# The order and the width of the twelve matmuls of a weight slot

## The chip, the cores and the metric

The kernel runs on one core of a Trainium2 chip. The metric is the device time of one execution in microseconds (us). Several executions are made, and the median is taken. One further execution is profiled; all rows below are from that one.

## What is computed

The reference is the trunk of an encoder: four layers over 256 tokens of width 2048, with a cross-attention to 256 memory rows. Cut to what matters here:

```python
for i in range(DEPTH):                      # 4 layers
    h = rms_norm(x, norm_g[i])              # 256 x 2048
    z = h @ w_in                            # 2048 x (5632 or about 7168)
    mix_out = (gmlp, forgetting attention, differential attention)[i % 3](z)
    kv = mem_n @ w_mem_kv[i]                # 256 x 2048 @ 2048 x 1024
    mem_out = memory_attention(...)
    branch = concatenate([mix_out, mem_out]) * silu(gate)
    x = x + branch @ w_out[i]               # 2048 x 2048
```

All inputs are float32. Nearly all of the arithmetic lies in the three kinds of product with a weight matrix: `w_mem_kv`, `w_in` and `w_out`.

## The kernel before

**Chunks and slots.** Each weight matrix is cut into blocks of 512 output columns, the chunks. There are 74 of them in the program, numbered here from 0 in the order in which they run: 0 to 7 are the memory keys and values, 8 to 18 the input projection of layer 0, 19 to 22 its output projection, 23 to 36 and 37 to 40 those of layer 1, 41 to 54 and 55 to 58 those of layer 2, 59 to 69 and 70 to 73 those of layer 3. `chunk_product` (L148) runs one chunk. A chunk has eight slots; a slot is a weight tile of 128 partitions by 1024 elements, which holds two blocks of 128 rows of the matrix (`kk` is 0 or 1), each 512 columns wide.

**The split in three products.** Every float32 operand is split in two parts of the type float32r, a high one and a low one. ScalarE makes the high part of the weights (`whi`, L117), VectorE the low part (`wlo`, L118), for the slot that is four ahead. The activations lie transposed as `xh` and `xl` (for the input projections) or `bh` and `bl` (for the memory rows and the output projections). One product is then three matmuls, one per term: `xh` with `whi` (L173), `xh` with `wlo` (L174) and `xl` with `whi` (L175). The activations are the stationary operand, 128 by 128, and the weights are the moving operand, 512 columns. The 256 tokens make two token tiles (`t` is 0 or 1), each with its own accumulator `acc[t]`, one bank of PSUM. So a slot has 2 (`kk`) x 2 (`t`) x 3 (terms) = 12 matmuls, and the program has 74 x 8 x 12 = 7104 of them. Before each one the chip loads its stationary operand: the trace has one weight load (the row PEld) for each matmul (the row PE).

**What sets the order.** The order on each engine is the order in which the program issues (a manual schedule). Within a slot it is `for kk, t in order`, with the three terms innermost; in the last slot of a chunk (`n == 7`) `order` is sorted by `t`, so that `acc[0]` is complete six matmuls ahead of `acc[1]`. Between slots `between_slots` (L142) issues whatever else is due: transposes, small matmuls of the attention, the next weight load on SyncE's queue (`load_until`), the next split (`split_until`). Four raw tiles, four `whi` and four `wlo` are the buffers; a `whi` buffer comes free when the last matmul that reads it is done, and the ScalarE instruction that refills it waits for that.

**Other matmuls.** Transposes (L344, L551, L560, L611, L799), scores (L459, L476, L501) and the gating product (L677) are float32 matmuls that stand between slots. A float32 matmul is run by the chip in two passes, each with a record of its own. The forget gate (L714 to L716) is the one other place with float32r: its stationary operand has 12 columns and its moving operand 256.

Of the kernel before, what the change touches and what calls it, by code (L numbers as in the profile page):

```python
# [24 lines left out]
CW = 512  # L25
# [7 lines left out]
RAW_BUFS = 4  # L33
PART_BUFS = 4
WARM = 10
LAM_LAYER = 2
LAM_INIT = 0.8 - 0.6 * math.exp(-0.3 * LAM_LAYER)

# [4 lines left out]
def trunk_kernel(  # L43
# [23 lines left out]
    nc = tc.nc  # L67
# [26 lines left out]

    pieces = piece_sequence()
    raws, parts, first_raw = {}, {}, []
    state = {"slot": 0, "raw": 0, "part": 0}

    def load_until(n):
        while state["raw"] < min(n, len(pieces)):  # L100
# [28 lines left out]
    def tick():  # L129
        for gen in list(tasks):  # L130
            if next(gen, tasks) is tasks:
                tasks.remove(gen)
        tasks.extend(fresh)
        fresh.clear()

    def run_late():
        todo = list(late)
        late.clear()
        for fn in todo:
            fn()  # L140

    def between_slots():  # L142
        tick()
        split_until(state["slot"] + PART_BUFS)
        load_until(state["slot"] + PART_BUFS + RAW_BUFS)
        run_late()

    def chunk_product(parts_of):  # L148
        acc = [
            ps_acc.tile([P, CW], F32, tag="acc", name=f"acc{t}") for t in range(2)  # L150
        ]
        for n in range(8):
            between_slots()
            slot = state["slot"]
            kp = pieces[slot][1]
            guard = 0
            while parts_of(kp) is None:
                assert (tasks or fresh) and guard < 100
                tick()
                run_late()  # L160
                guard += 1
            xh, xl = parts_of(kp)
            hi, lo = parts.pop(slot)
            order = [(kk, t) for kk in range(2) for t in range(2)]
            if n == 7:
                order.sort(key=lambda o: o[1])
            for kk, t in order:
                first = n == 0 and kk == 0
                last = n == 7 and kk == 1
                wh = hi[:, kk * CW : (kk + 1) * CW]  # L170
                wl = lo[:, kk * CW : (kk + 1) * CW]
                c = slice(kk * S + t * P, kk * S + (t + 1) * P)
                nc.tensor.matmul(acc[t], xh[:, c], wh, start=first, stop=False)  # L173
                nc.tensor.matmul(acc[t], xh[:, c], wl, start=False, stop=False)  # L174
                nc.tensor.matmul(acc[t], xl[:, c], wh, start=False, stop=last)  # L175
            state["slot"] += 1
        return acc


# [7 lines left out]
    warm_ps = ps_t.tile([P, CW], F32, tag="t", name="warm_ps")  # L187
    for _ in range(WARM):
        nc.tensor.matmul(warm_ps, warm[:, :P], warm, start=True, stop=True)
# [18 lines left out]
    def transposed_load(src, kp):  # L208
        raw = tmp.tile([P, 2 * S], F32, tag="xo", name="xraw", bufs=4)
        nc.sync.dma_start(raw, src[kp])  # L210
        return raw
# [21 lines left out]
    raw = tmp.tile([P, 2 * S], F32, tag="xo", name="xraw", bufs=4)  # L233
    m_hi, m_lo = new_parts("b", 0)
    bparts[0] = (m_hi, m_lo)
    for k in range(2):
        nc.sync.dma_start(raw[:, k * S : (k + 1) * S], mem_t[0, :, k * S : (k + 1) * S])
        w = slice(k * CW, (k + 1) * CW)
        nc.sync.dma_start(w_raw[:, w], pieces[0][0][0, :, w])
    for k in range(2):  # L240
        c, w = slice(k * S, (k + 1) * S), slice(k * CW, (k + 1) * CW)
# [3 lines left out]
    for kp in range(1, early):  # L245
        raw = transposed_load(mem_t, kp)
# [115 lines left out]
    for i in range(DEPTH):  # L362
        acc = chunk_product(lambda kp: bparts[kp])
        vv = heads.tile([P, 2, CW], F32, tag="vv", name="mvv")

        def store_values(i=i, acc=acc, vv=vv):
            scaled_rows(acc, r_mem, vv)
            nc.gpsimd.dma_start(mv_d[i], vv.rearrange("p a b -> p (a b)"))

        if i == 0:  # L370

            def first_values():
                yield from token_rms(mem, r_mem)
                yield
                store_values()

            spawn(first_values())
        else:
            store_values()
        if i == 2:  # L380
            spawn(load_transposed(x_t, "x", 0, xparts))
        if i == 3:
            spawn(token_rms(x, r_x))
        acc = chunk_product(lambda kp: bparts[kp])
        kt = heads.tile([P, 4, S], F32, tag="kT", name="mkt")

        def store_keys(i=i, kt=kt):
            nc.gpsimd.dma_start(mk_d[i], kt.rearrange("p a b -> p (a b)"))

        spawn(norm_task(acc, r_mem, gains[:, G_MK + i : G_MK + i + 1], HD, kt, store_keys))  # L390
# [415 lines left out]
    for i in range(DEPTH):  # L806
# [9 lines left out]
        def product():  # L816
            return chunk_product(lambda kp: xparts[kp])
# [26 lines left out]
        if kind == 0:  # L844
# [3 lines left out]
            for c in range(3):  # L848
                acc = product()
# [9 lines left out]
            for c in range(3):  # L859
                acc = product()  # L860
# [6 lines left out]
        else:  # L867
# [10 lines left out]
            for c in range(3):  # L878
                ready = []
                acc = product()  # L880
                qt = heads.tile([P, 4, S], F32, tag="qT", name="qt")
                spawn(norm_task(acc, r_x, qgains[:, gq : gq + 1], width, qt))
                acc = product()
# [11 lines left out]
                acc = product()  # L895
# [27 lines left out]
        for n in range(4):  # L923
            xo = old_rows(i, n)
            acc = chunk_product(lambda kp: bnext[kp])
# [90 lines left out]
```

## Time and profile before

| what | value |
|---|---|
| median of 3 runs | 1813.2 us (1813.01 to 1814.32) |
| the profiled execution: its time | 1813.01 us |
| its span (first to last instruction) | 1810.9 us |
| what lies around the span | 2.1 us |
| PE busy | 1791.0 us, 99% of the span |
| DVE busy / ACT busy | 1020.9 us / 905.4 us |
| mean granted TensorE clock | 0.994 |

PE is TensorE's matmul row, PEld its weight loads, which overlap it; DVE is VectorE, ACT ScalarE, POOL GpSimd, SP SyncE. A matmul's recorded duration reaches beyond the start of the next one, since matmuls are pipelined: the pace at which they run is read from start to start, not from the duration.

### The profile page before, as it was taken

The page shows a single profiled execution, that of the slowest core. Times are in us where ns is not written, and L with a number is a line of the kernel's source. Part 1 is how long each engine was busy: PE and PEld are TensorE (multiplying, and loading weights), DVE is VectorE, ACT ScalarE, POOL GpSimd, SP SyncE. Part 2 cuts the span into 40 slices and gives each one's busy share as a digit, 9 for nine tenths or more (in the row PEclk, how much of TensorE's full clock was granted, in tenths as well). Part 3 has the DMA queues.
Part 4 walks back from the last instruction along what each step waited for, and adds up shares of the span by engine and source line. Part 5 has one row for each costly group of instructions (what it writes and reads, how often), then busy time and mean ns, then how long its engine had stood idle before and what let it go on. Part 6 is the DMA issues. An engine that isn't in the chain of part 4 may idle for free.

```text
span 1810.9 us, 22215 instructions
## 1 busy us (share of the span) xinstructions
PE 1791.0 (99%) x8290; PEld 1465.7 (81%) x8290; DVE 1020.9 (56%) x1431; ACT 905.4 (50%) x1273; POOL 113.4 (6%) x131
## 2 busy tenths in 40 slices
PE   8999999999899999999999999999999999999999
PEld 6888888887688888888888887878888888888887
DVE  5456557554455555555555555766565555755454
ACT  5546545543455545455544454555464444554432
POOL 0110100000000110000000100101000000100000
PEclk9999999999899999999999999999999999999999
DMA  8767765556776455555566645454546766545564
GB/s 273 269 224 264 248 218 178 185 177 158 201 232 218 163 178 183 165 173 175 197 218 229 204 161 188 153 172 161 177 151 216 230 222 222 166 163 182 185 221 164
DMA packets 103932, 355.97 MB, mean 197 GB/s; under 512 B 12064, under 2 KB 12364, under 8 KB 103696
## 3 DMA queue, kind: packets, MB, share of 16 engines
q1 hardware_dynamic: 97344, 332.97, 55.3%
q0 software_dynamic: 5760, 20.50, 4.0%
q8 instruction: 65, 1.06, 0.3%
q10 hardware_dynamic: 720, 1.09, 0.2%
q14 instruction: 43, 0.35, 0.1%
HBM read 339.55 MB, written 14.95 MB: 196 GB/s over the span
## 4 chain that ended last, share of the span: by engine, by line
PE 96%; DMA 3%; ACT 0%; DVE 0%; issue 0%; SPq 0%; ACTq 0%; DVEq 0%
PE acc L173 30%; PE acc L175 29%; PE acc L174 29%; PE tb L551 2%; DMA raw<-in_w_o_dram 2%; PE tb L344 1%; PE tb L560 1%; PE tb L611 1%; PE s L459 1%; PE s L501 1%; PE tb L799 1%; PE sv L677 1%; DMA xraw<-in_mem_t_dram 1%; DMA raw<-in_w_kv_dram 1%; PE s L476 0%; ACT whi L117 0%
## 5 line engine op out<-in xcount | busy, mean ns | idle before, releaser
L118 DVE TENSOR_TENSOR wlo<-raw,whi 128x1024 fp32r<-128x1024 f32 x591 | 722.8, 1224 | 629.8 <-ACT whi L117 623.5
L117 ACT CAST whi<-raw 128x1024 fp32r<-128x1024 f32 x591 | 619.3, 1048 | 544.0 <-PE acc L175 472.8
L173 PE MATMUL acc<-whi,xh 128*128 128x512 f32 x1600 | 647.1, 404 | 2.6 <-ACT whi L117 2.6
L175 PE MATMUL acc<-whi,xl 128*128 128x512 f32 x1600 | 629.1, 393 | 0.0
L174 PE MATMUL acc<-wlo,xh 128*128 128x512 f32 x1600 | 625.0, 391 | 0.8 <-DVE wlo L118 0.8
L175 PEld LDWEIGHTS acc<-whi,xl 128*128 128x128 f32 x1600 | 300.9, 188 | 68.9
L173 PEld LDWEIGHTS acc<-whi,xh 128*128 128x128 f32 x1600 | 301.4, 188 | 67.3 <-issue 3.2
L174 PEld LDWEIGHTS acc<-wlo,xh 128*128 128x128 f32 x1600 | 301.5, 188 | 62.4 <-DVE wlo L118 1.1
L173 PE MATMUL acc<-whi,bh 128*128 128x512 f32 x768 | 306.2, 399 | 6.3 <-ACT whi L117 3.5
L174 PE MATMUL acc<-wlo,bh 128*128 128x512 f32 x768 | 303.5, 395 | 2.8 <-DVE wlo L118 1.8
L175 PE MATMUL acc<-whi,bl 128*128 128x512 f32 x768 | 301.5, 393 | 0.4 <-DVE bl L199 0.4
L173 PEld LDWEIGHTS acc<-whi,bh 128*128 128x128 f32 x768 | 145.4, 189 | 39.8 <-ACT whi L117 5.3
L174 PEld LDWEIGHTS acc<-wlo,bh 128*128 128x128 f32 x768 | 145.6, 190 | 34.0 <-DVE wlo L118 3.1
L175 PEld LDWEIGHTS acc<-whi,bl 128*128 128x128 f32 x768 | 145.4, 189 | 33.1 <-DVE bl L199 1.1
L307 POOL TENSOR_TENSOR sc<-sc,expo 128x8 f32<-128x8 f32 (+1 forms) x23 | 56.8, 2469 | 543.7 <-DVE sc L306 477.4
L564 ACT COPY pt<-tb 128x256 f32<-128x256 f32 (+1 forms) x80 | 27.2, 340 | 125.5 <-PE tb L560 125.3
L199 DVE SCALAR_TENSOR_TENSOR xl<-tb,gk,xh 128x256 fp32r<-128x256 f32 x48 | 23.2, 484 | 29.5 <-ACT xh L198 29.4
L198 ACT ACTIVATE xh<-tb,gk 128x256 fp32r<-128x256 f32 x48 | 22.8, 475 | 32.6 <-PE tb L799 19.4
L615 ACT CAST bh<-tb 128x512 fp32r<-128x512 f32 x26 | 15.3, 588 | 47.5 <-PE tb L611 47.5
L781 POOL DMA_DIRECT2D x_d<-xn x24 | 13.1, 547 | 358.3 <-DVE xn L777 357.5
L464 DVE TENSOR_REDUCE st<-s 128x1 f32<-128x256 f32 x32 | 13.6, 424 | 32.3 <-PE s L459 32.3
L574 DVE TENSOR_SCALAR mo<-tb,st 128x128 f32<-128x128 f32 x56 | 19.4, 346 | 19.3 <-ACT pt L564 16.5
(160 smaller groups left out, 955.9 us busy)
## 6 DMA issues: line engine op xcount, KB each, us to landing
raw<-in_w_a_dram SPq DMA_DIRECT2D x176, 512.0 KB, 3.3
raw<-in_w_o_dram SPq DMA_DIRECT2D x128, 512.0 KB, 4.1
raw<-in_w_b_dram SPq DMA_DIRECT2D x112, 512.0 KB, 3.2
raw<-in_w_c_dram SPq DMA_DIRECT2D x112, 512.0 KB, 3.2
raw<-in_w_kv_dram SPq DMA_DIRECT2D x63, 512.0 KB, 4.2
x_d<-xn POOLq DMA_DIRECT2D x24, 256.0 KB, 6.4
xo<-x_d SPq DMA_DIRECT2D x24, 256.0 KB, 5.4
lnp<-in_ln_dram SPq DMA_DIRECT2D x12, 256.0 KB, 6.0
```

Of the source, the lines that this page charges most:

```text
L117: nc.scalar.copy(hi, raw)
L118: nc.vector.tensor_sub(lo, raw, hi.bitcast(F32))
L173: nc.tensor.matmul(acc[t], xh[:, c], wh, start=first, stop=False)
L174: nc.tensor.matmul(acc[t], xh[:, c], wl, start=False, stop=False)
L175: nc.tensor.matmul(acc[t], xl[:, c], wh, start=False, stop=last)
L198: nc.scalar.activation(hi, src, AF.Copy, scale=g)
L199: nc.vector.scalar_tensor_tensor(lo, src, g, hi.bitcast(F32), ALU.mult, ALU.subtract)
L307: nc.gpsimd.tensor_tensor(sc[:, :, :n], sc[:, :, :n], expo.rearrange("p (a b) -> p a b", a=2)[:, :, :n], ALU.pow,)
L344: nc.tensor.transpose(tb[:, i, :], qn[t][:, i * P : (i + 1) * P], ident)
L551: nc.tensor.matmul(av, pt[:, j * P : (j + 1) * P], vv[:, j, f], start=(j == 0), stop=(j == tiles(t) - 1),)
L564: nc.scalar.copy(pt[:, : nk * P], tb[:, : nk * P])
L574: nc.vector.tensor_scalar(mo[t][:, f], av, done_st[:, 2:3], None, ALU.mult)
```

## The change

A table `FORMS` gives each chunk a form by its number modulo 10; the first and the last slot of every chunk keep the form "term". The function `slot_order` makes the list of the matmuls of one slot.

- "term" (16 of 74 chunks): the order before, three terms of one `kk` and `t` after each other.
- "bank" (22 chunks): for each `kk` and term first `acc[0]`, then `acc[1]`.
- "moving" (22 chunks): the four matmuls that stream `whi` first, then the two that stream `wlo`.
- "pair" (7 chunks: 6, 16, 26, 36, 46, 56, 66): the order of "term", but each matmul is two of 256 columns, one after the other.
- "half" (7 chunks: 9, 19, 29, 39, 49, 59, 69): all twelve on columns 0 to 255, then all twelve on columns 256 to 511.

So 44 chunks x 6 slots x 12 = 3168 matmuls stand in another order, and in 14 chunks x 6 slots = 84 slots there are 24 matmuls in place of 12, that is 1008 more matmuls, each with its own weight load.

```diff
+FORMS = ("term", "bank", "moving", "term", "bank", "moving", "pair", "moving", "bank", "half")
...
+    def slot_order(form, final):
+        full = slice(0, CW)
+        halves = (slice(0, CW // 2), slice(CW // 2, CW))
+        kts = [(kk, t) for kk in range(2) for t in range(2)]
+        if final:
+            kts.sort(key=lambda o: o[1])
+        if form == "term":
+            return [(kk, t, m, full) for kk, t in kts for m in range(3)]
+        if form == "bank":
+            return [(kk, t, m, full) for kk in range(2) for m in range(3) for t in range(2)]
+        if form == "moving":
+            return [
+                (kk, t, m, full)
+                for kk in range(2)
+                for t, m in ((0, 0), (0, 2), (1, 0), (1, 2), (1, 1), (0, 1))
+            ]
+        if form == "pair":
+            return [(kk, t, m, part) for kk, t in kts for m in range(3) for part in halves]
+        return [(kk, t, m, part) for part in halves for kk, t in kts for m in range(3)]
...
+            form = FORMS[state["chunk"] % len(FORMS)]
+            if n in (0, 7):
+                form = "term"
+            for kk, t, m, part in slot_order(form, n == 7):
+                w = (hi, lo, hi)[m]
+                xx = (xh, xh, xl)[m]
                 c = slice(kk * S + t * P, kk * S + (t + 1) * P)
-                nc.tensor.matmul(acc[t], xh[:, c], wh, start=first, stop=False)
-                nc.tensor.matmul(acc[t], xh[:, c], wl, start=False, stop=False)
-                nc.tensor.matmul(acc[t], xl[:, c], wh, start=False, stop=last)
+                lead, end = n == 0 and kk == 0 and m == 0, n == 7 and kk == 1 and m == 2
+                nc.tensor.matmul(
+                    acc[t][:, part], xx[:, c], w[:, kk * CW + part.start : kk * CW + part.stop],
+                    start=lead, stop=end,
+                )
```

In the listings of the program below, a row is line, operation, output<-moving operand,stationary operand, and the size; the number behind a name is that of the buffer. TensorE, first half (`kk` 0) of the second slot of chunk 2, before:

```order
L173 MATMUL acc0_545<-whi_504,bh1_125 128x512
L174 MATMUL acc0_545<-wlo_505,bh1_125 128x512
L175 MATMUL acc0_545<-whi_504,bl1_126 128x512
L173 MATMUL acc1_546<-whi_504,bh1_125 128x512
L174 MATMUL acc1_546<-wlo_505,bh1_125 128x512
L175 MATMUL acc1_546<-whi_504,bl1_126 128x512
```

The same place now, in the form "moving":

```order
L193 MATMUL acc0_545<-whi_504,bh1_125 128x512
L193 MATMUL acc0_545<-whi_504,bl1_126 128x512
L193 MATMUL acc1_546<-whi_504,bh1_125 128x512
L193 MATMUL acc1_546<-whi_504,bl1_126 128x512
L193 MATMUL acc1_546<-wlo_505,bh1_125 128x512
L193 MATMUL acc0_545<-wlo_505,bh1_125 128x512
```

The same six matmuls stand there; `whi` is read by the first four, and `wlo`, not `whi`, by the last.

TensorE, first half of the second slot of chunk 6, before:

```order
L173 MATMUL acc0_1247<-whi_1198,bh1_125 128x512
L174 MATMUL acc0_1247<-wlo_1199,bh1_125 128x512
L175 MATMUL acc0_1247<-whi_1198,bl1_126 128x512
L173 MATMUL acc1_1248<-whi_1198,bh1_125 128x512
L174 MATMUL acc1_1248<-wlo_1199,bh1_125 128x512
L175 MATMUL acc1_1248<-whi_1198,bl1_126 128x512
```

The same place now, in the form "pair" ("x2" marks two instructions that read alike: the two halves):

```order
L193 MATMUL acc0_1247<-whi_1198,bh1_125 128x256 x2
L193 MATMUL acc0_1247<-wlo_1199,bh1_125 128x256 x2
L193 MATMUL acc0_1247<-whi_1198,bl1_126 128x256 x2
L193 MATMUL acc1_1248<-whi_1198,bh1_125 128x256 x2
L193 MATMUL acc1_1248<-wlo_1199,bh1_125 128x256 x2
L193 MATMUL acc1_1248<-whi_1198,bl1_126 128x256 x2
```

Each matmul has become two of half the width on the same stationary operand.

VectorE in the first "moving" chunk (2), with the counters for which each instruction waits in brackets (PE_49 is raised by TensorE, Activation_49 by ScalarE, DMAHW by the weight loads), before:

```order
L118 TENSOR_TENSOR wlo_591<-raw_508,whi_590 128x1024 [waits DMAHW0_49,Activation_49]
L321 TENSOR_TENSOR qn_608<-acc0_368,sc_553 128x512 [waits Pool_49]
L321 TENSOR_TENSOR qn_610<-acc1_369,sc_553 128x512 [waits Pool_49]
L118 TENSOR_TENSOR wlo_613<-raw_526,whi_612 128x1024 [waits DMAHW1_49,Activation_49]
L118 TENSOR_TENSOR wlo_637<-raw_551,whi_636 128x1024 [waits DMAHW2_49,PE_49,Activation_49]
```

And now:

```order
L119 TENSOR_TENSOR wlo_591<-raw_508,whi_590 128x1024 [waits DMAHW0_49,PE_49,Activation_49]
L343 TENSOR_TENSOR qn_608<-acc0_368,sc_553 128x512 [waits Pool_49]
L343 TENSOR_TENSOR qn_610<-acc1_369,sc_553 128x512 [waits Pool_49]
L119 TENSOR_TENSOR wlo_613<-raw_526,whi_612 128x1024 [waits DMAHW1_49,PE_49,Activation_49]
L119 TENSOR_TENSOR wlo_637<-raw_551,whi_636 128x1024 [waits DMAHW2_49,PE_49,Activation_49]
```

The order is the same; the subtraction that makes `wlo` now also waits for TensorE itself, where before it needed only ScalarE's cast. On ScalarE, GpSimd and SyncE's queue no instruction moves.

## Rows read from the trace of the kernel before

**Rows 1.** The head of the profile's page: the span, busy time by engine (share of the span, instructions), and the granted TensorE clock in 40 slices, in tenths of full speed.

```profile
span 1810.9 us, 22215 instructions
PE 1791.0 (99%) x8290; PEld 1465.7 (81%) x8290; DVE 1020.9 (56%) x1431; ACT 905.4 (50%) x1273; POOL 113.4 (6%) x131
PEclk9999999999899999999999999999999999999999
PE 96%; DMA 3%; ACT 0%; DVE 0%; issue 0%; SPq 0%; ACTq 0%; DVEq 0%
```

**Rows 2.** The view of waits: engine and line, what it waited for, us in total, times, the longest.

```profile
PE acc L173 <- ACT whi L117: 6.1, 4, 2.6
PE acc L174 <- DVE wlo L118: 2.5, 4, 0.8
...
DVE wlo L118 <- ACT whi L117: 623.5, 479, 11.2
...
ACT whi L117 <- PE acc L175: 472.8, 303, 3.1
```

**Rows 3.** The timeline of TensorE in chunk 60 (whose form is "term"): start, duration (us), operation, count. The first matmul, the starts of the second slot, the third and the last, and that of chunk 61.

```profile
1480.38 0.39 PE L173 MATMUL acc<-whi,xh 128*128 128x512 f32 x1
...
1483.12 0.40 PE L173 MATMUL acc<-whi,xh 128*128 128x512 f32 x1
...
1485.87 0.39 PE L173 MATMUL acc<-whi,xh 128*128 128x512 f32 x1
...
1499.60 0.39 PE L173 MATMUL acc<-whi,xh 128*128 128x512 f32 x1
...
1502.35 0.39 PE L173 MATMUL acc<-whi,xh 128*128 128x512 f32 x1
```

**Rows 4.** The same view at the start of chunk 2, whose stationary operands are `bh` and `bl`: the starts of its first, second and third slot.

```profile
58.35 0.39 PE L173 MATMUL acc<-whi,bh 128*128 128x512 f32 x1
...
61.07 0.39 PE L173 MATMUL acc<-whi,bh 128*128 128x512 f32 x1
...
63.79 0.39 PE L173 MATMUL acc<-whi,bh 128*128 128x512 f32 x1
```

**Rows 5.** The timeline of TensorE in the forget gate: four rows of the first twelve matmuls of 256 columns, the first three and the last.

```profile
645.22 0.28 PE L714 MATMUL z<-xh,fh 128*12 128x256 f32 x1
645.34 0.28 PE L715 MATMUL z<-xl,fh 128*12 128x256 f32 x1
645.45 0.28 PE L716 MATMUL z<-xh,fl 128*12 128x256 f32 x1
...
646.48 0.28 PE L716 MATMUL z<-xh,fl 128*12 128x256 f32 x1
```

**Rows 6.** The groups of instructions of the weight loads (PEld) by shape: line, operation, operands, stationary columns, count, then busy us and mean ns of one, idle us before them.

```profile
L174 PEld LDWEIGHTS acc<-wlo,xh 128*128 128x128 f32 x1600 | 301.5, 188 | 62.4 <-DVE wlo L118 1.1
...
L715 PEld LDWEIGHTS z<-xl,fh 128*12 128x12 f32 x16 | 1.5, 91 | 0.6
```

**Rows 7.** The timeline of TensorE, matmuls and weight loads, in a plain stretch of an input projection.

```profile
641.10 0.39 PE L173 MATMUL acc<-whi,xh 128*128 128x512 f32 x1
641.10 0.19 PEld L174 LDWEIGHTS acc<-wlo,xh 128*128 128x128 f32 x1
...
641.33 0.39 PE L174 MATMUL acc<-wlo,xh 128*128 128x512 f32 x1
641.33 0.19 PEld L175 LDWEIGHTS acc<-whi,xl 128*128 128x128 f32 x1
```

**Rows 8.** Two pieces of the chain that ended last (start, us, what), with float32 passes: L459 has 256 columns a pass, L677 has 128, and every pass its own weight load of 128 columns.

```profile
310.45 0.43 PE s L459 x2
310.88 0.89 PE sv L677 x8
```

**Rows 9.** The timeline of the weight loads behind those passes, where the slot's own loads follow.

```profile
311.50 0.19 PEld L173 LDWEIGHTS acc<-whi,xh 128*128 128x128 f32 x1
311.61 0.19 PEld L174 LDWEIGHTS acc<-wlo,xh 128*128 128x128 f32 x1
```

**Rows 10.** The chain in layer 2, the scores of the differential attention: four passes of 256 columns on half the partitions.

```profile
1135.70 0.63 PE s L501 x4
```

**Rows 11.** The longest stall, at the end of chunk 18 and the start of chunk 19: a row of the view by windows (window, us, busy us and count of PE, PEld, DVE, ACT, POOL, granted clock, share of the DMA engines and GB/s), then the timeline of TensorE with the idle time before a matmul and what ended it in brackets.

```profile
455.00:460.00 5.00, 4.65 (x11) 3.47 (x11) 0.29 (x1) 0.05 (x1) 0.00 (x0) 0.50 0.87 162
```

```profile
454.09 0.50 PE L173 MATMUL acc<-whi,xh 128*128 128x512 f32 x1 [2.62 <-ACT whi L117]
455.35 0.79 PE L174 MATMUL acc<-wlo,xh 128*128 128x512 f32 x1 [0.76 <-DVE wlo L118]
...
456.36 0.63 PE L173 MATMUL acc<-whi,xh 128*128 128x512 f32 x1
456.79 0.63 PE L174 MATMUL acc<-wlo,xh 128*128 128x512 f32 x1
...
461.05 0.79 PE L173 MATMUL acc<-whi,bh 128*128 128x512 f32 x1 [0.65 <-ACT whi L117]
...
468.01 0.72 PE L173 MATMUL acc<-whi,bh 128*128 128x512 f32 x1 [1.81 <-ACT whi L117]
```

**Rows 12.** The costliest groups on the page: VectorE's subtraction and ScalarE's cast (line, operation, operands, count, then busy us and mean ns of one, idle us before them and what ended most of it).

```profile
L118 DVE TENSOR_TENSOR wlo<-raw,whi 128x1024 fp32r<-128x1024 f32 x591 | 722.8, 1224 | 629.8 <-ACT whi L117 623.5
L117 ACT CAST whi<-raw 128x1024 fp32r<-128x1024 f32 x591 | 619.3, 1048 | 544.0 <-PE acc L175 472.8
```

More of the change, by code (lines that the diff above doesn't have):

```diff
@@ L96, in trunk_kernel @@
     raws, parts, first_raw = {}, {}, []
-    state = {"slot": 0, "raw": 0, "part": 0}
+    state = {"slot": 0, "raw": 0, "part": 0, "chunk": 0}
     def load_until(n):
@@ L163, in chunk_product @@
             hi, lo = parts.pop(slot)
[L164 to L171, printed above, removed]
-                c = slice(kk * S + t * P, kk * S + (t + 1) * P)
-                nc.tensor.matmul(acc[t], xh[:, c], wh, start=first, stop=False)
-                nc.tensor.matmul(acc[t], xh[:, c], wl, start=False, stop=False)
-                nc.tensor.matmul(acc[t], xl[:, c], wh, start=False, stop=last)
+            form = FORMS[state["chunk"] % len(FORMS)]
[4 more added lines that the diff above has]
+                xx = (xh, xh, xl)[m]
+                c = slice(kk * S + t * P, kk * S + (t + 1) * P)
+                lead, end = n == 0 and kk == 0 and m == 0, n == 7 and kk == 1 and m == 2
[3 more added lines that the diff above has]
+                )
             state["slot"] += 1
+        state["chunk"] += 1
         return acc
```

## The prediction

> **What bounds the kernel now.** I read the head of the page first. PE is busy for 1791.0 of 1810.9 us, 96% of the chain that ended last lies on it, and the granted clock is at its upper level, 2.4 GHz, in nearly every slice [rows 1]. The view of waits says the same from the other side: the two largest waits of the matmuls sum to 8.6 us over the whole program, while VectorE and ScalarE wait for hundreds of us, ScalarE above all for TensorE to free a `whi` buffer [rows 2]. So the kernel takes as long as its matmuls take to start one after another, and the only question about the change is the pace from start to start, in each of the five orders.
>
> The pace comes from the timeline. In a plain chunk, six slots of 12 matmuls run from 1483.12 to 1499.60 us: 16.48 us / 72 = 228.9 ns each. The last slot, 1499.60 to 1502.35, gives 2.75 / 12 = 229.2 ns [rows 3]. In the first two slots of chunk 2 it is 5.44 us / 24 = 226.7 ns [rows 4]. These are the two paces of a 512-column float32r matmul that the trace has; they differ by 2.2 ns. The duration of 0.39 us in the same rows is no pace, since each matmul starts long before the one ahead of it has ended.
>
> **The change part by part.**
>
> *Bank and moving (3168 matmuls in another order).* The number of matmuls, their width, and the number of weight loads stay. What changes is what stands next to each other, and the order before already holds each kind of neighbour: L173 to L174 keeps the stationary operand and the bank and changes the moving tile; L174 to L175 keeps the bank and changes both operands; L175 to the next L173 changes the stationary operand and the bank and, at the change of `t`, keeps the moving tile. In the last slot of a chunk six matmuls in a row go to one bank, in the others three, and the pace is 229.2 against 228.9 ns, equal within the 0.01 us to which a row is given [rows 3]. Reloading an unchanged stationary operand saves nothing now either: L174 has a load of its own in all 1600 cases, of the same 188 ns [rows 6]. I take 0. From both sides: if the new orders moved all 3168 matmuls to the pace of 226.7 ns, that would be 3168 x 2.2 ns = -7.0 us; if they lost as much again, +7.0 us.
>
> *Pair and half (84 slots with 24 matmuls of 256 columns for 12 of 512).* Now a slot costs 12 x 228.9 = 2747 ns; then it costs 24 p, where p is the pace of a 256-column float32r matmul with a full weight load ahead of each. No row shows that, so p is bounded. Below: half of the better pace, 113.3 ns [rows 4], so 2720 ns. Nearest row: the forget gate streams 256 columns of the same type, from 645.22 to 646.48 us in 11 steps, 114.5 ns each [rows 5]. So a narrow matmul as such pays no fixed price: 24 x 114.5 = 2748 ns, even. But its stationary operand has 12 columns, and here 128 must be loaded. The load is recorded with 91 ns for 12 columns and 188 for 128 [rows 6], (188 - 91) / 116 = 0.84 ns a column, so 107 ns of the 188 are the 128 columns, an estimate. It begins together with the matmul ahead of it [rows 7], and two float32r loads of 128 columns have followed each other after 0.11 us [rows 9]. So a load needs some 107 to 110 ns and has 113 to 114: it fits, with little to spare. Where every step is filled by a load, float32 passes of 128 columns run at 0.89 / 8 = 111.3 ns, while half a pass of 256 columns is 0.43 / 4 = 107.5 ns [rows 8]: up to 3.8 ns for the full load, and p = 114.5 + 3.8 = 118.3 at the upper end of what is near. A far row, scores on half the partitions, has 0.63 / 4 = 157.5 ns for 256 columns [rows 10].
>
> I take p = 113.3 + 2.2 = 115.5 ns, that is, I count the 2.2 ns by which the common pace lies above the better one once for each weight load and not once for 512 columns. It lies between the forget gate's 114.5 and 118.3, nearer to the first. Then a slot costs 24 x 115.5 = 2772 ns, 25 to 26 more than now, and 84 slots make **+2.2 us**. The ends: p = 113.3 gives -27 ns x 84 = -2.3 us, p = 118.3 gives 92 ns x 84 = +7.7 us, the far row 1033 ns x 84 = +87 us.
>
> By the Trainium skill, page "TensorE: Matmul & The Clock Gate", section "Back-to-back issue gap", a warm matmul takes its columns at 2.4 GHz plus a fixed 2.5 ns; by that, cutting a matmul in two costs 2.5 ns, 1008 times, +2.5 us. The trace does not have its 215.8 ns for 512 columns but 226.7 to 228.9, and whether the surplus comes with each matmul no run here shows.
>
> *Buffers.* In "moving" the last reader of `whi` is the tenth matmul of a slot and that of `wlo` the twelfth, so `wlo` comes free 2 x 229 = 458 ns after `whi`. VectorE's subtraction, which now waits for TensorE too, stands behind ScalarE's cast of the same slot, which takes 1048 ns [rows 12] and can't begin before `whi` is free; the new wait is over first. Behind it on VectorE are the other splits and the attention's work; all of it is for slots some 8 us ahead, and VectorE is idle 44% of the time [rows 1]. In "bank" the case is the reverse, and `whi` is free as late as now. I take 0. If that cover were gone, a slot would gain a wait of at most 458 ns on VectorE, still off the path.
>
> *The stall in chunks 18 and 19.* TensorE waits there for the casts of late weights, at the lower clock of 1.2 GHz [rows 11]. The matmuls at 454.09 and 461.05 us open a last and a first slot, which keep "term". The one at 468.01 opens the second slot of chunk 19, now "half": its second matmul needs `wlo` after 256 columns rather than 512, so up to half of the 0.43 us between two starts there is waited out rather than covered: +0.2 us once, within rounding.
>
> **Sum.** The profiled execution took 1813.01 us (1810.9 in the span, 2.1 around it), 0.2 below the median of the three runs, so the two are interchangeable here: 1813.0 + 0 + 2.2 + 0 + 0.1 = **1815.3 us**, +0.13%. A measurement of this kernel can tell about 0.2% from no change, 3.6 us. So I forecast no change that can be told.
>
> **The rivals.**
>
> *A, slower: the load sets the pace of the narrow matmuls.* With 113 ns to hide a load of 107 to 110 ns, any handover of more than a few ns comes on top 24 times a slot. For it: the 111.3 ns of L677 against 107.5 [rows 8]. Against it: 0.11 us between loads in rows 9. It decides from 3.6 us / 84 = 43 ns a slot, p = 116.2 ns, less than 1 ns above what I took. At p = 118.3 the time is 1813.0 + 7.7 = 1820.7 us.
>
> *B, much slower: loads are not hidden.* If a load could not run under a matmul, each of the 1008 new ones would add its 107 ns, +108 us, 1921 us. Against it: loads that start in the same 0.01 us as the matmul ahead [rows 7], and matmuls 228.9 ns apart, with no room for 107 ns behind 213 (512 columns at 2.4 GHz). The Trainium skill, the same page, section "The mechanism", says that a weight load overlaps a matmul in flight only if it goes to another row group, which the loads here, over all 128 rows, do not; by that rule B would hold, and the trace disagrees.
>
> *C, faster: the order carries the 2.2 ns.* If what costs 228.9 rather than 226.7 ns is a neighbourhood that "bank" and "moving" remove, 7.0 us go: 1813.0 - 7.0 + 2.2 = 1808.2 us. For it: the better pace exists. Against it: the chunk that shows it runs the same order as all the others [rows 3, 4]. The mirror case, orders that cost 2.2 ns more, gives 1822.3 us.
>
> **How the numbers follow.** The forecast 0.55; A with the mirror case of C 0.30; B or the far row 0.04; C 0.11. The range leaves out B, part of C and the outermost of A: 1808.5 to 1821.5 us. Faster by over 0.2% is C alone, 0.10; slower is A, its mirror and B, 0.34; the rest, 0.56, lies within.
>
> **What would show it.** In the profile of the changed kernel the starts in a "bank" or "moving" slot should still be 228 to 230 ns apart, a slot 2.75 us; the chunks with "pair" or "half" should have 24 starts in 2.75 to 2.79 us, with 1008 more records on PE and on PEld. A slot of 2.84 us there is A, 3.8 us or more is B; 2.72 us in "bank" or "moving" is C. The prediction is wrong in its grounds if waits on `wlo` appear in "moving" chunks, or if "pair" and "half" differ, since I see no reason for a difference between the two.

## The result and the profile after

The changed kernel takes 1816.81 us (median of 14 runs, 1815.28 to 1819.55) against 1813.58 us for the kernel before on the same chip (14 runs, 1811.63 to 1815.46). The ratio is 1.0018, with a 95% interval of 1.0010 to 1.0026: +3.2 us where +2.2 was forecast. The interval does not reach 1, so the change can be told, which the prediction had not expected. The profiled execution took 1817.74 us.

The head of its page, with span and busy time by engine (share, instructions):

```profile
span 1815.6 us, 24233 instructions
...
PE 1796.4 (99%) x9298; PEld 1515.0 (83%) x9298; DVE 1021.3 (56%) x1431; ACT 905.4 (50%) x1273; POOL 113.7 (6%) x131
```

Against [rows 1] there are 1008 records more on PE and on PEld, as many as there are new matmuls; TensorE still bounds the kernel, and its span is 4.7 us longer. The other engines did the same work. The view of waits, as in [rows 2]:

```profile
PE acc L193 <- ACT whi L118: 6.7, 4, 2.8
PE acc L193 <- DVE wlo L119: 2.7, 4, 0.8
...
DVE wlo L119 <- ACT whi L118: 620.6, 470, 11.0
...
ACT whi L118 <- PE acc L193: 468.2, 301, 3.2
```

No new kind of wait appears. The subtraction that now names TensorE among its releasers has no row of waiting for it.

So the time lies in the pace. The timeline of TensorE in chunk 61 ("bank") and chunk 62 ("moving"): the starts of the second and third slot of 61, the first and second of 62, and its last.

```profile
1508.78 0.62 PE L193 MATMUL acc<-whi,xh 128*128 128x512 f32 x2
...
1511.52 0.62 PE L193 MATMUL acc<-whi,xh 128*128 128x512 f32 x2
...
1528.00 0.39 PE L193 MATMUL acc<-whi,xh 128*128 128x512 f32 x1
...
1530.75 0.39 PE L193 MATMUL acc<-whi,xh 128*128 128x512 f32 x1
...
1547.23 0.39 PE L193 MATMUL acc<-whi,xh 128*128 128x512 f32 x1
```

A "bank" slot takes 2.74 us, and the six "moving" slots from 1530.75 to 1547.23 us take 16.48, like the six of [rows 3]: 228.9 ns a matmul. Summed over the program, the 132 "bank" and the 132 "moving" slots take 0.3 us less than the same slots before. The narrow slots look different. Chunk 16 ("pair") has its third and fourth slot between transposes; each row below is two narrow matmuls:

```profile
389.81 0.40 PE L193 MATMUL acc<-whi,xl 128*128 128x256 f32 x2
390.05 0.40 PE L193 MATMUL acc<-whi,xh 128*128 128x256 f32 x2
...
391.93 0.40 PE L193 MATMUL acc<-whi,xl 128*128 128x256 f32 x2
392.17 0.60 PE L633 MATMUL tb<-ident,br 128*128 128x128 f32 x4
392.52 0.48 PE L193 MATMUL acc<-whi,xh 128*128 128x256 f32 x2
...
393.06 0.39 PE L193 MATMUL acc<-whi,xl 128*128 128x256 f32 x2
...
395.10 0.39 PE L193 MATMUL acc<-whi,xl 128*128 128x256 f32 x2
```

From 389.81 to 391.93 there are 9 rows, 18 matmuls: 117.8 ns each. From 393.06 to 395.10 there are again 9: 113.3 ns. The matmuls, the tiles and the operands are alike; a transpose stands between. Over all 84 narrow slots (pace from the third matmul to the last of the slot), 22 run as a whole at 113.3 ns, 54 at 117.8 (the fast and the slow rhythm below), 6 at 119 to 120, and 2 stand in the stall. The six are the slots on `bh1` and `bh2`. Against 2747 ns for a slot before, that is 22 x -28 + 54 x 80 ns, and six times about 140 ns against the 2720 to 2750 ns of those slots: -0.6 + 4.3 + 0.8 = +4.5 us.

Read from slot start to slot start, these 82 slots take 4.2 us more than before. The rest of the 4.7 us by which the span grew is two differences that nearly cancel: chunk 0 takes 1.0 us less, and the third slot of chunk 19, in the stall, 1.6 us more (4.81 for 3.20 us). In that slot the granted clock falls to its lower level, where before it stayed up. The view by windows, before and then now, with the clock third from the end:

```profile
477.00:481.00 4.00, 4.00 (x21) 3.29 (x20) 2.21 (x3) 2.33 (x4) 0.00 (x0) 1.00 0.76 247
```

```profile
477.00:481.00 4.00, 4.00 (x24) 4.00 (x23) 1.83 (x2) 1.03 (x2) 0.00 (x0) 0.57 0.66 206
```

Just ahead of it TensorE had waited 1.4 to 1.5 us for VectorE in both. The narrow matmuls need not be the cause: in e4 and e5 below, whose matmuls there are 512 columns wide, some in the same slot start 427 ns apart, and in e12, where they are narrow, the slot keeps the upper level.

### The profile page after: what moved, and what is told of

Its sections match the earlier page's. It is cut to its first block, busy times and chain, and to the rows that moved or that the text cites. A ratio compares the mean times of both kernels' runs of the same rounds, so it can differ in the third digit from the quotient of the medians.

```text
span 1815.6 us, 24233 instructions
## 1 busy us (share of the span) xinstructions
PE 1796.4 (99%) x9298; PEld 1515.0 (83%) x9298; DVE 1021.3 (56%) x1431; ACT 905.4 (50%) x1273; POOL 113.7 (6%) x131
## 4 chain that ended last, share of the span: by engine, by line
PE 96%; DMA 2%; ACT 0%; issue 0%; DVE 0%; SPq 0%; ACTq 0%; DVEq 0%
PE acc L193 89%; PE tb L573 2%; DMA raw<-in_w_o_dram 2%; PE tb L366 1%; PE tb L582 1%; PE tb L633 1%; PE s L481 1%; PE s L523 1%; PE tb L821 1%; PE sv L699 1%; DMA raw<-in_w_kv_dram 0%; PE s L498 0%; DMA xraw<-in_mem_t_dram 0%; ACT whi L118 0%; DVE wlo L119 0%
## 5 line engine op out<-in xcount | busy, mean ns | idle before, releaser
L193 PE MATMUL acc<-whi,xh 128*128 128x512 f32 (+1 forms) x1840 | 635.4, 373 | 2.4 <-ACT whi L118 2.4
L193 PE MATMUL acc<-whi,xl 128*128 128x512 f32 (+1 forms) x1840 | 617.0, 363 | 0.0
L193 PE MATMUL acc<-wlo,xh 128*128 128x512 f32 (+1 forms) x1840 | 589.3, 363 | 0.5 <-DVE wlo L119 0.5
L193 PEld LDWEIGHTS acc<-whi,xl 128*128 128x128 f32 x1840 | 337.5, 188 | 56.3
L193 PEld LDWEIGHTS acc<-wlo,xh 128*128 128x128 f32 x1840 | 337.7, 188 | 55.4 <-DVE wlo L119 1.0
L193 PEld LDWEIGHTS acc<-whi,xh 128*128 128x128 f32 x1840 | 335.0, 188 | 58.4 <-issue 3.8
L193 PE MATMUL acc<-whi,bh 128*128 128x512 f32 (+1 forms) x864 | 303.0, 373 | 6.1 <-ACT whi L118 4.2
L193 PE MATMUL acc<-whi,bl 128*128 128x512 f32 (+1 forms) x864 | 299.1, 369 | 0.4 <-DVE bl L221 0.4
L193 PE MATMUL acc<-wlo,bh 128*128 128x512 f32 (+1 forms) x864 | 284.2, 370 | 2.8 <-DVE wlo L119 2.2
L193 PEld LDWEIGHTS acc<-wlo,bh 128*128 128x128 f32 x864 | 161.3, 191 | 31.2 <-DVE wlo L119 3.1
L221 DVE SCALAR_TENSOR_TENSOR xl<-tb,gk,xh 128x256 fp32r<-128x256 f32 x48 | 23.2, 484 | 29.8 <-ACT xh L220 29.5
L317 ACT ACTIVATE sq<-acc,r_x 128x512 f32<-128x512 f32 x32 | 22.1, 690 | 18.0 <-PE acc L193 17.8
```

Source lines behind the costliest of these rows:

```text
L193: nc.tensor.matmul(acc[t][:, part], xx[:, c], w[:, kk * CW + part.start : kk * CW + part.stop], start=lead, stop=end,)
L221: nc.vector.scalar_tensor_tensor(lo, src, g, hi.bitcast(F32), ALU.mult, ALU.subtract)
L317: nc.scalar.activation(sq, src[t], AF.Square, scale=rcols[:, t : t + 1])
```

## The experiments

Two questions were open: what the narrow matmul's surplus over 113.3 ns is, and whether the order may gain or cost. Each ratio is to the kernel before in the same session. The edits of e1 to e4, e6 and e10 to e12 are to the changed kernel, the others to the kernel before. The profile of each is one execution.

**e1 and e2, one narrow form everywhere.**

```diff
-FORMS = ("term", "bank", "moving", "term", "bank", "moving", "pair", "moving", "bank", "half")
+FORMS = ("pair",)        # e1
+FORMS = ("half",)        # e2
```

> Every chunk has the form pair in its six inner slots (444 slots in place of 42 with pair). In the changed kernel's trace a narrow slot runs as a whole at 113.3 ns from start to start or at 117.7, 38 misaligned pair slots in the ratio 16 to 22. Theory 1 (the weight load of 128 columns needs nearly the whole narrow step, and the two settle in one of two rhythms): both rhythms again, a mean near 116 ns, 444 x (24 x 116 - 2747) = +16 us over the kernel before, 1830 us; 1801 if all slots took the fast one, 1849 if all took the slow one. Rival (a narrow matmul as such has a fixed price): one pace for all slots, 116.3 ns, +20 us.

> Every chunk has the form half in its six inner slots. In the changed kernel 32 of 38 misaligned half slots ran at 117.7 ns and 6 at 113.3. If the order of the halves decides on the rhythm, half stays slower than pair: 444 x (24 x 117.1 - 2747) = +28 us, 1842 us, some 12 us over pair for all. If the rhythm is chance or the place in the program, the two kernels agree within 4 us.

Measured: e1 1831.56 us, ratio 1.0107 (1.0091 to 1.0123); e2 1831.52 us, 1.0106 (1.0088 to 1.0124). Both rhythms appear again, so there is no one price of a narrow matmul. Outside the slots on `bh0` to `bh2` and the stalls, e1 and e2 agree on the rhythm in all 394 slots that can be compared, 155 fast and 239 slow. So the order of the halves does nothing to the rhythm. The place alone does not fix it either: of the 76 narrow slots of the changed kernel outside `bh0` to `bh2`, 61 have the rhythm that e1 has at the same place and 15 the other one. Nor does the place account for "half" being slower than "pair" there: in e1 the places of the seven "pair" chunks have 10 fast slots of 38 and those of the seven "half" chunks 11. What ran ahead is left as the reason, which is not shown. In e1 the rhythm stayed from one slot to the next in 194 of 195 cases where nothing came between, and changed in 37 of 127 where other matmuls did, so the 38 slots of a form are far fewer separate draws. The slots on `bh1` and `bh2` are at 120 ns in both.

**e3, half the weight load.** e1 with a stationary operand of 64 columns in the inner slots.

```diff
+                rows = slice(0, P if form == "term" else P // 2)
+                c = slice(c.start, c.start + rows.stop)
                 nc.tensor.matmul(
-                    acc[t][:, part], xx[:, c], w[:, kk * CW + part.start : kk * CW + part.stop],
+                    acc[t][rows, part], xx[:, c], w[:, kk * CW + part.start : kk * CW + part.stop],
```

> As pair for all, but in the six inner slots the stationary operand has 64 columns, not 128: the products of the upper 64 tokens of each token tile are left out there. Columns streamed, number of matmuls and of loads stay; only a load is half as long. Theory 1 (the load): the slow rhythm goes, all narrow slots at 113.3 to 113.8 ns, 444 x (24 x 113.4 - 2747) = -11 us against the kernel before, 1802 us. Rival (a price of the narrow matmul): as pair for all, 1830 us with both rhythms.

Measured: 1823.36 us, 1.0063 (1.0047 to 1.0078): neither of the two. The load is shorter, as its group in the view by shapes shows:

```profile
L195 PEld LDWEIGHTS acc<-whi,xh 128*64 128x64 f32 x2400 | 299.5, 134 | 10.6 <-issue 2.2
L195 PEld LDWEIGHTS acc<-whi,xh 128*128 128x128 f32 x400 | 75.6, 189 | 18.7 <-ACT whi L118 2.5 <-issue 1.0 <-ACT u L688 0.6
```

134 ns for 64 columns lie between the 91 and 188 of [rows 6], as a fixed part and 0.84 ns a column would have it. But only the slots on `bh1` and `bh2` went from 120 to 113.5 ns. Of the others 67 ran at 113.3 and 327 at 116.7 ns, which is 1.1 ns less than the slow rhythm with twice the load. There was no gain there: 88 slots that were fast in e1 have become slow, and the mean of these 394 slots is 116.1 ns in e3 and 116.0 in e1. The 48 slots on `bh1` and `bh2` alone make up most of the 8.2 us between e1 and e3 (48 x 24 x 6.5 ns = 7.5 us). So my first theory, that the load has no room, agrees with `bh0` to `bh2` and falls for the rest.

**e4, the order alone.** `FORMS = ("bank", "moving")`.

> No narrow matmuls; bank and moving alternate over all 74 chunks, 5328 matmuls in another order. If the order costs nothing: 228.9 to 229.2 ns in both forms, within 2 us of the kernel before. If one of the orders removes or adds the 2.2 ns: up to 12 us faster or slower.

Measured: 1813.5 us, 1.0007 (0.9998 to 1.0017). Nearly all slots have 226.5 to 230.5 ns, most of them 228.9, in both forms and as in the kernel before. Order is free within the interval, 0.4 us less to 3.1 us more.

What sets `bh0` to `bh2` apart is their address, which e9 tests below. In the addresses that the built program gives its tiles, the weight tiles and these six stationary tiles stand a multiple of 512 bytes apart; the row factors, three buffers of 64 bytes, lie behind them and push every later `bh`, `bl`, `xh` and `xl` tile 192 bytes off.

**e5 to e8, other distances.** The row factors' pad moves the stationary operands, e8 moves weights and stationary operands together.

```diff
-ROW_PAD = 16
+ROW_PAD = 32             # e5, and e6 with FORMS = ("pair",)
+ROW_PAD = 24             # e7
...
-    expo = const.tile([P, 16], F32, name="expo")
+    expo = const.tile([P, 32], F32, name="expo")[:, :16]      # e8
```

> The kernel before with one constant changed: the pad of the row factors from 16 to 32 words moves every bh, bl, xh and xl tile behind them by 192 bytes, so that these stationary operands start at the same place within 128 bytes as the weight tiles do (32), as only bh0 to bh2 did. Theory 2 (the 2.2 ns depend on where the stationary operand starts against the moving one): 226.5 ns in all slots, about 6400 matmuls x 2.3 ns = -14 us, 0.992 of the kernel before. Rival (the better pace of the first slots has to do with the chunk or the stretch): no change.

> Pair for all with the same pad of 32. In pair for all the aligned narrow slots ran at 120 ns, the others at 113.3 or 117.7, and with the short load the aligned ones at 113.5. Theory 2 with the load's length (aligned, a narrow matmul waits out its load; at 512 columns the load is hidden): all 444 inner slots at 120 ns, 24 x 120 - 12 x 226.5 = +162 ns a slot, +72 us over the aligned kernel before, about 1870 us. Rival (the place in the chunk): the same mix as pair for all, 1831 us.

> The kernel before with a pad of 24 words: the stationary operands behind it start at 64 within 128 bytes, 32 away from the weight tiles' 32, where the kernel before has 64 away. If equal starts alone are good, the pace stays at 228.9 ns or changes to another surplus, within 0.3% of the kernel before; if any distance but 64 will do, 226.5 ns as in the aligned kernel, -14 us.

> The kernel before with 64 bytes more in the constants, which moves weight tiles and stationary operands together: weights at 96, stationary operands behind the row factors at 32, bh0 to bh2 at 96. If the distance between the two decides: paces as before, 226.5 ns with bh0 to bh2 and 228.9 elsewhere, no change in time. If the stationary operand's own place decides: 226.5 ns nearly everywhere, -14 us.

Measured: e5 1833.34 us, 1.0113 (1.0098 to 1.0128); e6 1860.45 us, 1.0264 (1.0248 to 1.0279); e7 1836.6 us, 1.0133 (1.0117 to 1.0148); e8 1809.01 us, 0.9987 (0.9977 to 0.9996). The second theory, in the form that the starts within 128 bytes count, falls with e5: equal there, and slower by 21 us. But the distance does count, and the matmuls' pace is where it shows. The second and third slot of chunk 60 in e5:

```profile
1497.40 0.40 PE L173 MATMUL acc<-whi,xh 128*128 128x512 f32 x1
...
1500.20 0.40 PE L173 MATMUL acc<-whi,xh 128*128 128x512 f32 x1
```

2.80 us a slot, 233.3 ns by the whole chunk, against 2.75 in [rows 3]; e7 has 2.80 as well, 233.3 ns. In e5 and e7 the slots on `bh1` and `bh2`, not moved, keep their 226.7 ns where they follow another slot directly (23 of 26 in each, 23 of 26 before). e8, with all tiles moved and the distance kept, has the paces of the kernel before. Its 3.3 us less don't come from them: in its profile chunk 0, which waits for the first weights, takes 27.7 us where that of before took 31.2. (In the profiles of e4, e5, e7 and e9 it takes 28.4 to 29.8, so this start varies between profiles.)

**e9 to e12, distance zero.** The row factors come from another pool, so that all stationary tiles stand a multiple of 512 bytes from the weight tiles.

```diff
-        return act.tile([P, ROW_PAD], F32, tag="r", name=name, bufs=3)[:, :2]
+        return small.tile([P, ROW_PAD], F32, tag="r", name=name, bufs=3)[:, :2]
```

e9 is the kernel before with this edit, e10 has `FORMS = ("pair",)` too, e11 the short load of e3 as well, e12 is the changed kernel with it.

> The kernel before with the row factors taken from another pool, so that all bh, bl, xh and xl tiles stand a whole multiple of 512 bytes from the weight tiles, as bh0 to bh2 alone did (the two experiments with pads of 24 and 32 words put them 288 and 384 bytes past a multiple, and the paces became 233.5 and 232 to 234 ns; before it is 192 past, 228.9 ns). Theory 3 (the distance between stationary and moving operand within 512 bytes sets the surplus over 226.7 ns, and zero is free): 226.5 to 227 ns in all slots, some 6400 x 2.2 ns = -14 us, 0.992 of the kernel before. Rival (the first slots of a chunk are fast for another reason): 228.9 ns or more outside them, no gain.

> Pair for all in the same layout. The narrow slots with bh0 to bh2 ran at 120 ns. Theory 3: all narrow slots at 120 ns, (24 x 120 - 12 x 226.7) x 444 = +71 us over the kernel of this layout without narrow matmuls, about 1870 us. Rival: the mix of 113.3 and 117.7 ns outside the first slots, some 1830 us.

> Pair for all in the same layout, with a stationary operand of 64 columns in the inner slots (the products of the upper 64 tokens of each token tile are left out there). With bh0 to bh2 the short load took the pace from 120 to 113.5 ns. If the surplus of 6.7 ns in this layout is the load that does not fit in the step: 113.3 to 113.5 ns in all narrow slots, no more than 1800 us. If it is the layout's price for a narrow matmul: 117 to 120 ns, 1840 to 1870 us.

> The changed kernel in the same layout. Theory 3: 3168 matmuls in other orders at 226.7 ns, free as before; the 84 narrow slots at 24 x 120 ns instead of 12 x 226.7, +160 ns each, +13 us over the kernel of this layout without the change, near 1811 us and so about the time of the kernel before. Rival: as in the old layout, +3 us over whatever that kernel takes.

Measured: e9 1800.12 us, 0.9937 (0.9925 to 0.9950); e10 1863.55 us, 1.0284 (1.0268 to 1.0300); e11 1800.09 us, 0.9937 (0.9924 to 0.9951); e12 1813.26 us, 1.0010 (1.0001 to 1.0019). Chunk 60 once more, the starts of the second and third slot and of the last, in e10 and in e11:

```profile
1525.09 0.40 PE L193 MATMUL acc<-whi,xh 128*128 128x256 f32 x2
...
1527.97 0.40 PE L193 MATMUL acc<-whi,xh 128*128 128x256 f32 x2
...
1542.37 0.40 PE L193 MATMUL acc<-whi,xh 128*128 128x512 f32 x1
```

```profile
1473.10 0.40 PE L195 MATMUL acc<-whi,xh 128*64 128x256 f32 x2
...
1475.82 0.39 PE L195 MATMUL acc<-whi,xh 128*64 128x256 f32 x2
...
1489.42 0.40 PE L195 MATMUL acc<-whi,xh 128*128 128x512 f32 x1
```

With the full load a narrow slot takes 2.88 us, 120.0 ns a matmul; with half the load 2.72 us, 113.3 ns. And with 512 columns and the full load, in e9, the first, second and last slot:

```profile
1469.84 0.39 PE L173 MATMUL acc<-whi,xh 128*128 128x512 f32 x1
...
1472.56 0.39 PE L173 MATMUL acc<-whi,xh 128*128 128x512 f32 x1
...
1488.88 0.39 PE L173 MATMUL acc<-whi,xh 128*128 128x512 f32 x1
```

2.72 us, 226.7 ns a matmul. The third theory's times were met within 7 us, and its paces wherever slots follow one another. In e9, of the 396 inner slots outside `bh1` and `bh2`, 246 follow another slot directly, and 245 of them run at 226.7 ns (before: 244 at 228.9). The other 150 come behind transposes or other matmuls and run at 227 to 232 ns, all but one. Their mean of 229.3 ns hardly differs from the 229.6 of before, which the theory did not foresee; e9 gained 11.5 us where 14 was expected. The change costs 13.1 us in this layout (e12 less e9), where 13 was expected from 84 slots at 160 ns; in the layout that it was made in it cost 3.2.

The paces by distance of the stationary tile, modulo 512 bytes, ahead of the weight tile, worked out from the starts of all inner slots:

| distance | 512 columns | 256 columns, load of 128 | 256 columns, load of 64 |
|---|---|---|---|
| 0 (e9 to e12; `bh0` to `bh2` everywhere) | 226.7 ns, 227 to 232 behind other matmuls | 119 to 120 ns | 113.3 to 114 ns in most slots |
| 192 (the kernel before, the changed one) | 228.9 ns, up to 233 behind other matmuls | 113.3 or 117.8 ns | 113.3 or 116.7 ns |
| 288 (e7) | 232 to 233.5 ns | not run | not run |
| 384 (e5, e6) | 231.5 to 234 ns | 118.5 to 119 ns in most slots | not run |

## Why the prediction was right, point by point

*TensorE's pace bounds the kernel.* Right; the differences of the runs lie in the main in the pace inside the slots. The start and the stall move too: over all profiles chunk 0 takes 27.7 to 31.2 us, and the third slot of chunk 19 takes 3.2 to 5.6.

*Bank and moving cost nothing.* Right, by the paces in the changed kernel and by e4, where all 74 chunks have them. The argument, that the order before already holds each kind of neighbour, has a gap: in "moving" the first two matmuls keep both the moving operand and the bank and change the stationary operand alone, which the order before has nowhere. The runs show that this neighbour is free too. Rival C, that an order might remove the 2.2 ns, had a surplus that can be removed, but not by order: e9 removes most of it by an address.

*Pair and half cost 84 x (24 x 115.5 - 2747).* The mechanism was right in part, the size off. The term that was mis-sized is p: 115.5 ns, taken as half of 226.7 ns and 2.2 ns for the load. The mean of the 82 slots outside the stall is (22 x 113.3 + 54 x 117.8 + 6 x 119.7) / 82 = 116.7 ns, and the term came to +4.2 to +4.5 us in the profile rather than +2.2. No slot ran at 115.5: there are separate rhythms, both ends of the near range, 113.3 and 118.3, were nearly met, and their mixture made the mean. By the prediction's own signs rival A came nearer than the forecast says: A was to decide from 116.2 ns, and 54 of the 82 slots take 24 x 117.8 ns = 2.83 us, where 2.84 was its sign. That much hangs on the load in the step is what distance zero speaks for: with a full load each narrow matmul takes 6.7 ns more, with half a load mostly 0 to 0.7. But half a load is also half the columns of the array and half the rows of the accumulator, and no run separates these from the load's length. At the distance of 192 bytes, where the forecast was made, half the load took 1.1 of 4.4 ns off the slow rhythm and gained nothing in the mean, so there the surplus does not follow the load's length.

That the forecast came so near is partly luck. The prediction had one pace and no tile addresses; the mean of two rhythms happened to lie 1.2 ns above it. With the tiles 192 bytes elsewhere the same change costs 13.1 us, which on 1813.0 us would have been 1826, outside the range. The far row was no pace either: the four passes of L501 behind +87 us start in pairs 6 to 8 ns apart, two side by side.

*No reason for pair and half to differ.* Right, by e1 and e2, though the changed kernel's own profile suggests otherwise: 32 of 38 against 22 of 38 slow slots. Why it has that split is open.

*Buffers and the stall.* Buffers: right, no new wait. The stall: put at +0.2 us, which the sum carries as 0.1; it came to +1.6 us in the profile, by the lower clock and not by the wait on `wlo` that the prediction had. *Rival B*, loads exposed: excluded; 1008 loads cost 3.2 us, some 3 ns each and not 107.

*What stays open.* Why a distance of 192 bytes has two rhythms for 256 columns and one for 512, what sets the rhythm at the entry of a slot, and by what mechanism the distance acts. Only four distances were run; whether the pattern repeats after 512 bytes or after 256 they can't tell (after 128 it does not: 0 and 384 differ). Each edit of the layout moved attention tiles as well, whose matmuls hardly changed their pace. Why slots behind other matmuls stay at 227 to 232 ns in e9 is open.

## What to carry to other kernels

When matmuls run back to back with a fresh stationary operand each, halving the moving width doubles the weight loads, and whether they still hide has to be read from the start-to-start pace, slot by slot: a mean over two rhythms hides both. Look at the places where the same instruction runs at two paces in the same trace; here that clue, 226.7 against 228.9 ns, led to the tiles' addresses, and one line that takes three small buffers out of the pool (e9) is worth 0.6%, more than three times what the change costs, and beats both kernels. Reordering the same matmuls was worth nothing.

## What the runs showed of the hardware that was not expected

- The pace of a float32r matmul depends on the distance between the addresses of its two SBUF operands: 226.7, 228.9, 233 to 233.5 and 231.5 to 234 ns for 512 columns at 0, 192, 288 and 384 bytes modulo 512 (e9, the kernel before, e7, e5), in slots that follow one another directly. Moving both by 64 bytes changes no pace (e8).
- Two rhythms for the same narrow matmul, 113.3 and 117.8 ns, that hold for whole slots and can change where other matmuls come between. They were the same at 394 of 394 places in e1 and e2, which differ in the order of the halves, but at only 61 of 76 in e1 and the changed kernel.
- The distance that is best for 512 columns is the worst that was run for 256: 120 ns, 6.7 ns over half of 226.7 (e10).
